# Two ordering edits in the first mixer of a hybrid decoder trunk: where a pair's normalised keys stand on VectorE, and when the second half's cosines and sines are loaded and scaled

## The chip, the cores and the metric

The kernel runs on one core of one Trainium2 chip. The metric is device time in microseconds (us) of one execution. The profile is one further execution under the hardware profiler, whose span runs from the first to the last instruction of the program.

## The reference, cut to what matters

The reference is a decoder trunk of two layers on a sequence of 1024 tokens with 1024 features, all in float32. The first layer mixes with two groups of heads: eight retention heads (rotary q and k) and eight RWKV-7 heads. Only that first mixer is touched.

```python
z = h @ w_in                                 # h = rms_norm(x)
q, k, v, g = jnp.split(z_ret, 4, axis=-1)    # retention heads
q = rotary(heads(q), pos)                    # x1*cos - x2*sin, x1*sin + x2*cos
k = rotary(heads(k), pos) * HEAD_DIM ** -0.5
o = chunk_retention(q, k, heads(v))
...
kkf = heads(kr * k_k)                        # RWKV heads: normalised keys
kk = kkf / jnp.maximum(jnp.linalg.norm(kkf, axis=-1, keepdims=True), 1e-12)
...
y = rwkv7_scan(r_h, heads(decay), k_h, v_h, -kk, kk * heads(a))
```

`rwkv7_scan` goes token by token; the kernel does it in chunks of 64 tokens, with a short recurrence from chunk to chunk. After the mixer come its output projection, a SwiGLU FFN, a layer of sliding-window attention with its own FFN, and a final norm.

## The kernel before

Features lie on the 128 partitions and tokens along the free axis, in two halves of 512 tokens. The RWKV heads go in pairs (two heads of 64 features fill 128 partitions). So (0,3) is the fourth pair of the first half, and a unit is two pairs of one half: units 0 and 1 are the first half's pairs 0, 1 and 2, 3; units 2 and 3 are the second half's.

**Projections.** A projection job is 24 matmuls of 128x512: eight slices of the features, three products each, since activations and weights are split into a rounded high part and a remainder (`n` and `w` in the profile). ScalarE makes a weight's high part (L335), in the mixer VectorE makes its remainder (L336). The activations `n` of the second half are made by `gained`: ScalarE multiplies a slice by its gain and rounds it (L469), VectorE makes the remainder (L470), for each of eight slices. The factor 1/rms (`rs`) is not in `n`; it is multiplied in when a result leaves PSUM. For the rotary projections it is multiplied into the cosines and sines instead, on GpSimd (L485 for the first half, L585 for the second).

**Rotary.** When a rotary projection (`retk`, `retq`) is done, ScalarE copies it out (L1013), four small DMAs fetch a copy with the halves swapped (L1017), GpSimd multiplies by the cosines (L1018), VectorE the copy by the sines (L1019) and adds them (L1020). The tiles `c_cos` and `c_sin` have one buffer each, so the second half's can be loaded only when the first half's last rotation has read the old ones.

**The second half's norm.** `second_norm` loads x, sums its squares and makes `rs` (L572, L573). Then it waits for the event `g0_3`, the end of the first half's last projection, loads the eight slices of x again (L579, four buffers `nq`), makes `n`, and last loads and scales cosines and sines. The second half's projections begin with `w1_0`.

**A pair.** `pair` makes the decays, the inverse norm of the keys (`rn`), and with L712 the normalised keys `kk`. Behind it on VectorE come seven more operations that need `kk` or what follows from it: L715, L716 (into AR), L717, L719, L723, L724 (into BK), L752. AR and BK feed a matmul whose masked result (L736) goes through DRAM into the unit's triangular inversion (L857 and L861, 31 steps of two small VectorE operations).

**The recurrence.** `unit` ends with eight steps, one for each chunk: eight small matmuls into one PSUM bank (`ps_c`), then for each of the two pairs one VectorE operation that writes the next state (L959). Matmuls of the outputs (`ps_m<-AR,GT`) use those states.

**What sets the order.** `Plan` is a planner in the kernel: it traces the pieces of these generators and the projection jobs in an order by estimated costs and due times; a `yield (("retq0_3", 1.0),), 0.0` means that a generator goes on one unit of the planner's clock behind the event `retq0_3`. The framework then orders each engine's and queue's instructions once more, ahead of time, by when their inputs are there in its own model; where several could go, the one traced first goes first. The order of each queue is then fixed. Two helpers tie it:

```python
def keep(self, i):
    return self.tc.keep_in_program_order(i)   # i goes behind the instruction traced just before it on its queue
def behind(self, i, first):                   # i goes behind first on their common engine
    self.tc.add_manual_dep(i.ins, first.ins.name, ...)
```

The eight loads of x at L579 are all tied with `keep`.

## Time and profile before

| | |
|---|---|
| time, median of 3 runs | 2331.51 us (2331.47 to 2333.43) |
| time of the profiled execution | 2330.62 us |
| span of the profile | 2328.6 us (2.0 us of the time lie around it) |
| TensorE busy | 98% of the span |
| VectorE, ScalarE, GpSimd busy | 73%, 45%, 42% |
| matmuls of the first mixer | from 5.7 us to about 660 us of the span |

PE is TensorE, DVE VectorE, ACT ScalarE, POOL GpSimd, and SPq the queue of SyncE, which issues nearly all DMAs. A row of the timeline gives the start in us, the time that its instructions took in us (the merged ones together, where it ends with x2 and the like), engine, line and operation, what it writes and reads, and in brackets the engine's idle time before it and what ended that. A row of the waits gives who waited for whom, the total in us, how often, and the longest. A row of the windows gives, for a stretch of the span, each engine's busy time and instructions, then the granted TensorE clock as a share of full speed, and the share and rate of the DMA engines.

### The profile page before, as it was taken

What the parts mean: (1) busy time and instruction counts of PE and PEld (TensorE: products, weight loads), DVE (VectorE), ACT (ScalarE), POOL (GpSimd) and SP (SyncE); (2) the same over time, 40 slices, a digit from 0 to 9 for tenths busy, and PEclk for the clock granted to TensorE, in tenths of its full rate; (3) what the DMA queues carried; (4) which work ended last, traced back from release to release, by engine and by line L of the source; (5) the groups of instructions that cost most, each with busy time, mean ns of one, the idle gap of its engine ahead of it and who ended that gap; (6) DMA issues with size and microseconds to landing.
All of it is one profiled execution on the core that took longest, in us unless ns stands there. A gap on an engine that the chain in (4) does not pass through costs nothing.

```text
span 2328.6 us, 35662 instructions
## 1 busy us (share of the span) xinstructions
PE 2289.3 (98%) x13056; PEld 1816.4 (78%) x13056; DVE 1704.2 (73%) x2667; ACT 1044.2 (45%) x1943; POOL 979.8 (42%) x764
## 2 busy tenths in 40 slices
PE   8999999999999999999999999999999999999998
PEld 6777777777778888888788887777788888887886
DVE  6876865875667358888885957877647788888766
ACT  5454434424455333333343456666645333343335
POOL 3132221211341067777776500002102677776775
PEclk9999999999999999999999999999999999999999
DMA  7665553433445555555666331113236466656663
GB/s 276 207 210 194 189 152 127 138 119 112 148 173 191 201 167 207 209 208 214 249 257 216 107 127 64 57 64 122 96 128 224 159 222 218 214 200 252 249 217 113
DMA packets 170622, 407.46 MB, mean 175 GB/s; under 512 B 43216, under 2 KB 45904, under 8 KB 170448
## 3 DMA queue, kind: packets, MB, share of 16 engines
q1 hardware_dynamic: 167040, 398.63, 49.9%
q10 hardware_dynamic: 2832, 4.45, 0.5%
q8 instruction: 104, 1.70, 0.3%
q0 software_dynamic: 576, 2.10, 0.2%
q14 instruction: 70, 0.57, 0.1%
HBM read 276.53 MB, written 123.21 MB: 172 GB/s over the span
## 4 chain that ended last, share of the span: by engine, by line
PE 69%; DVE 5%; ACT 2%; issue 1%; POOL 0%; DMA 0%; DVEq 0%; POOLq 0%; ACTq 0%
PE ps_m L1191 7%; PE ps_m L1192 7%; PE ps_m L1193 7%; PE ps_f L350 4%; PE ps_f L351 4%; PE ps_f L352 4%; PE ps_f L1191 4%; PE ps_f L1193 4%; PE ps_f L1192 4%; PE ps_r L1191 2%; PE ps_r L1193 2%; PE ps_r L1192 2%; PE ps_c L1193 2%; PE ps_c L1192 2%; PE ps_c L1191 2%; PE ps_m L240 2%
## 5 line engine op out<-in xcount | busy, mean ns | idle before, releaser
L240 PE MATMUL ps_f<-n,w 128*128 128x512 f32 x1440 | 379.3, 411 | 8.9 <-ACT w L335 5.7
L240 PEld LDWEIGHTS ps_f<-n,w 128*128 128x128 f32 x1440 | 266.6, 190 | 91.4 <-issue 21.8
L336 POOL TENSOR_TENSOR w<-wr,w 128x512 fp32r<-128x512 f32 x63 | 85.9, 1368 | 523.9 <-ACT w L335 520.1
L335 ACT CAST w<-wr 128x512 fp32r<-128x512 f32 x231 | 142.1, 619 | 178.0 <-PE ps_f L352 76.7
L336 DVE TENSOR_TENSOR w<-wr,w 128x512 fp32r<-128x512 f32 x168 | 120.7, 722 | 68.2 <-ACT w L335 67.9
L336 POOL TENSOR_TENSOR w<-wq,w 128x512 fp32r<-128x512 f32 x91 | 130.3, 1442 | 31.9 <-ACT w L335 31.9
L1191 PE MATMUL ps_m<-n,w 128*128 128x512 f32 x333 | 130.9, 393 | 0.0
L1193 PE MATMUL ps_m<-n,w 128*128 128x512 f32 x333 | 130.2, 391 | 0.4 <-POOL w L1379 0.4
L1192 PE MATMUL ps_m<-n,w 128*128 128x512 f32 x333 | 130.1, 391 | 0.0
L350 PE MATMUL ps_f<-n,w 128*128 128x512 f32 x320 | 127.3, 399 | 0.0
L1200 DVE TENSOR_TENSOR nq<-ps_m,u 128x512 f32<-128x512 f32 x88 | 58.9, 684 | 93.3 <-PE ps_m L1193 93.3
L351 PE MATMUL ps_f<-n,w 128*128 128x512 f32 x320 | 126.9, 396 | 0.0
L352 PE MATMUL ps_f<-n,w 128*128 128x512 f32 x320 | 126.6, 396 | 0.0
L1191 PE MATMUL ps_f<-n,w 128*128 128x512 f32 x287 | 113.7, 396 | 0.0
L1193 PE MATMUL ps_f<-n,w 128*128 128x512 f32 x287 | 112.1, 392 | 0.0
L1192 PE MATMUL ps_f<-n,w 128*128 128x512 f32 x287 | 111.7, 389 | 0.0
L358 POOL TENSOR_TENSOR n<-nq,n 128x512 fp32r<-128x512 f32 x60 | 100.0, 1677 | 7.6 <-ACT n L356 7.6
L1379 POOL TENSOR_TENSOR w<-wd,w 128x512 fp32r<-128x512 f32 (+1 forms) x62 | 85.1, 1379 | 38.9 <-ACT w L1378 37.2
L1191 PE MATMUL ps_m<-cb,w 128*128 128x512 f32 x236 | 91.9, 389 | 0.3 <-DVE nq L1200 0.3
L1379 POOL TENSOR_TENSOR w<-ws,w 128x512 fp32r<-128x512 f32 (+1 forms) x48 | 71.8, 1502 | 47.8 <-ACT w L1378 47.8
L1192 PE MATMUL ps_m<-cb,w 128*128 128x512 f32 x236 | 91.8, 389 | 0.0
L1193 PE MATMUL ps_m<-cb,w 128*128 128x512 f32 x236 | 91.8, 389 | 0.0
(520 smaller groups left out, 6456.9 us busy)
## 6 DMA issues: line engine op xcount, KB each, us to landing
hc<-n SPq DMA_DIRECT2D x84, 512.0 KB, 2.8
wsp<-w SPq DMA_DIRECT2D x54, 512.0 KB, 3.4
w<-wsp SPq DMA_DIRECT2D x54, 512.0 KB, 3.5
n<-hc SPq DMA_DIRECT2D x54, 512.0 KB, 5.6
wq<-in_w_gate SPq DMA_DIRECT2D x44, 512.0 KB, 4.4
u<-u SPq DMA_DIRECT2D x88, 256.0 KB, 3.1
wr<-in_w_in SPq DMA_DIRECT2D x34, 512.0 KB, 4.9
ha<-hc SPq DMA_DIRECT2D x34, 512.0 KB, 5.7
```

The lines of the kernel that those rows point to most:

```text
L240: self.nc.tensor.matmul(out, lhsT, rhs, **kw)
L335: nc.scalar.copy(hi[:, :n], raw[:, c])
L336: self.lo.tensor_tensor(out=lo[:, :n], in0=raw[:, c], in1=hi.bitcast(F32)[:, :n], op=ALU.subtract)
L350: nc.tensor.matmul(ps, hi, rh, start=k == 0, stop=False)
L351: nc.tensor.matmul(ps, hi, rl, start=False, stop=False)
L352: nc.tensor.matmul(ps, lo, rh, start=False, stop=k == n - 1)
L358: e.tensor_tensor(out=lo, in0=src, in1=hi.bitcast(F32), op=ALU.subtract)
L1191: mm(ps, hi, xh, start=first and k == 0, stop=False, skip_group_check=True)
L1192: mm(ps, hi, xl, start=False, stop=False, skip_group_check=True)
L1193: mm(ps, lo, xh, start=False, stop=last and k == len(w) - 1, skip_group_check=True)
L1200: self.last_add = V.tensor_tensor(out=o, in0=x, in1=y, op=ALU.add)
L1379: nc.gpsimd.tensor_tensor(out=lo, in0=v, in1=hi.bitcast(F32), op=ALU.subtract)
```

## The change

`unit` keeps the last L959 instruction that was traced, of whichever unit and step, in `self.link`. `pair` ties its L712 behind that instruction on VectorE, if there is one. And `second_norm` loads and scales the second half's cosines and sines in a step of its own, one unit of the planner's clock behind `retq0_3` (the first half's last rotary projection) and ahead of its wait for `g0_3`, where they stood behind the eight slices of `n`.

```diff
-        self.h, self.plan = [None, None], None
+        self.h, self.plan, self.link = [None, None], None, None
...
         nc.scalar.activation(r, r, AF.Exp, scale=-0.5)
+        yield (("retq0_3", 1.0),), 0.0
+        cs = []
+        for nm in ("cos", "sin"):
+            c = self.const(self.rp, nm, (HT, HT), eng=nc.sync)
+            nc.gpsimd.tensor_tensor(out=c, in0=c, in1=r, op=ALU.mult)
+            cs.append(c)
         yield (("g0_3", 0.0),), 0.0
         n8 = self.n8(self.pp)
         self.nT = []
...
             self.keep(nc.sync.dma_start(x, self.A["xT"][k, :, HT:T]))
             self.nT.append(self.gained(x, "n1a", n8, k))
         self.rs = r
-        cs = []
-        for nm in ("cos", "sin"):
-            c = self.const(self.rp, nm, (HT, HT), eng=nc.sync)
-            nc.gpsimd.tensor_tensor(out=c, in0=c, in1=r, op=ALU.mult)
-            cs.append(c)
         self.cs = cs
...
-        V.scalar_tensor_tensor(out=kk, in0=k, scalar=self.col("kk", p), in1=rn, op0=ALU.mult, op1=ALU.mult)
+        i = V.scalar_tensor_tensor(out=kk, in0=k, scalar=self.col("kk", p), in1=rn, op0=ALU.mult, op1=ALU.mult)
+        if self.link is not None:
+            self.behind(i, self.link)
...
-                V.scalar_tensor_tensor(
+                self.link = V.scalar_tensor_tensor(
                     out=self.Srw[:, p, :] if c == NCH - 1 else GT[:, c + 1, :], in0=ps[:, q, :],
```

## The prediction

> **What bounds the kernel now.** I read the first lines of the page, then PE's waits, then windows around the two waits that the change can touch, and last each engine's timeline there.

> ```profile
> span 2328.6 us, 35662 instructions
> PE 2289.3 (98%) x13056; PEld 1816.4 (78%) x13056; DVE 1704.2 (73%) x2667; ACT 1044.2 (45%) x1943; POOL 979.8 (42%) x764
> PE ps_f L240 <- DVE n L470: 2.1, 1, 2.1
> PE ps_m L240 <- DVE GT L959: 2.0, 1, 2.0
> ```

> PE is the bound: 2289.3 of 2328.6 us. Neither edit removes a matmul, so all that can be won is PE's idle time and what hangs on it. Two of its longest waits are the ones that the edits touch: PE waited 2.0 us for a recurrence step (L959) and 2.1 us for a slice of the second half's activations (L470).

> ```profile
> 203.88:207.29 3.41, 1.79 (x29) 1.62 (x30) 3.38 (x8) 0.00 (x0) 0.00 (x0) 1.00 0.38 154
> 207.29:210.70 3.41, 3.41 (x8) 2.30 (x7) 1.80 (x5) 0.62 (x1) 0.00 (x0) 0.50 0.00 0
> 285.80:289.21 3.41, 1.50 (x15) 0.90 (x11) 3.41 (x4) 3.34 (x7) 3.04 (x3) 1.00 0.33 88
> 289.21:292.62 3.41, 3.17 (x8) 2.49 (x9) 3.41 (x7) 0.00 (x0) 0.00 (x0) 0.50 0.86 291
> ```

> Windows of 3.41 us: PE's busy time first, DVE's third, the granted clock third from the end. Each wait is followed by 3.41 us at half the clock. So a wait costs twice: the idle time, and the slow matmuls behind it.

> ```profile
> 206.51 3.56 PE L240 MATMUL ps_f<-n,w 128*128 128x512 f32 x9
> 209.87 1.44 PE L240 MATMUL ps_m<-rr,c_blk 128*128 128x512 f32 x2
> 220.89 5.28 PE L240 MATMUL ps_f<-n,w 128*128 128x512 f32 x22
> 226.01 1.02 PE L240 MATMUL ps_m<-rt,c_blk 128*128 128x512 f32 x2
> 289.45 5.40 PE L240 MATMUL ps_f<-n,w 128*128 128x512 f32 x16 [2.15 <-DVE n L470]
> ```

> A projection matmul takes 5.28/22 = 0.24 us at full clock. Nine would take 2.16 but took 3.56 in the first slow window, and the two of `c_blk` 1.44 where 1.02 is usual: 1.8 us lost. Behind the second wait 16 took 5.40 where 3.84 is due: 1.56 us. The first wait is thus worth 2.0 + 1.8 = 3.8 us, the second 2.15 + 1.56 = 3.7.

> [...]

> **Part 1, the keys.**

> ```profile
> 201.29 0.40 PE L240 MATMUL ps_c<-GT,XA 64*64 64x64 f32 x8
> 202.89 0.91 DVE L336 TENSOR_TENSOR w<-wr,w 128x512 fp32r<-128x512 f32 x1 [2.48 <-ACT w L335]
> 203.72 0.74 DVE L712 SCALAR_TENSOR_TENSOR rt<-rkk,pv,rt 128x512 f32<-128x512 f32 x1
> 204.49 0.68 DVE L715 TENSOR_TENSOR AR<-rt,rt 128x504 f32<-128x504 f32 x1
> 205.17 0.47 DVE L959 SCALAR_TENSOR_TENSOR GT<-ps_c,PC,XA 128x64 f32<-128x64 f32 x2
> 205.50 0.45 PE L240 MATMUL ps_m<-AR,GT 64*64 64x64 f32 x6 [2.01 <-DVE GT L959]
> 207.96 0.75 DVE L752 SCALAR_TENSOR_TENSOR rr<-rr,pv,rkk 128x512 f32<-128x512 f32 x1
> 222.35 0.46 DVE L959 SCALAR_TENSOR_TENSOR Srw<-ps_c,PC,XA 128x64 f32<-128x64 f32 x2
> ```

> The step's matmuls were over at 201.69; its DVE operation started at 205.17, because pair (0,3)'s L712 and L715 (and the short L716) stood in front. The planner traces that L712 behind all eight steps of unit 0, so the tie holds it behind the step of 222.35. On DVE the step now follows L336, which ends at 203.80. Its first operation ends 0.3 us later and PE goes on at about 204.1 in place of 205.50: -1.4 us. With that, the first window's PE time is 1.79 + 1.4 = 3.2 of 3.41, and I take the slow window as gone: -1.8. Bounds: 0, if another operation takes the keys' place, to -3.8.

> What is added is the wait of L712. Queued behind it are L715, L716, L717, L719, L723, L724 and L752, which with it held DVE from 203.72 to 208.71, less 0.47 for the step between them: 4.5 us that move to 222.8 or later. Who needs them:

> ```profile
> 222.00:236.00 14.00, 14.00 (x61) 9.91 (x60) 9.88 (x17) 7.05 (x13) 3.88 (x4) 1.00 0.66 223
> 240.10 1.15 PE L240 MATMUL ps_m<-AR,BK 64*64 64x64 f32 x32
> 245.98 1.02 PE L240 MATMUL ps_m<-rr,c_blk 128*128 128x512 f32 x2
> 366.11 0.75 DVE L712 SCALAR_TENSOR_TENSOR rt<-rkk,pv,rt 128x512 f32<-128x512 f32 x1 [0.57 <-ACT rt L704]
> 398.89 0.80 DVE L715 TENSOR_TENSOR AR<-rt,rt 128x504 f32<-128x504 f32 x1
> ```

> AR and BK are first multiplied at 240.10, L752's result at 245.98. DVE was busy 9.88 of the 14 us behind the last step, so 4.1 us are free there; the 4.5 us fit by about 229, eleven us ahead of their use. I cost this at nothing; if the cover is gone (a weight remainder L336 queued behind the keys) it is one more stop like that of 205.50, 3.8 us. The other pair that the tie can move is (1,1), whose L712 ran at 366.11, ahead of unit 1's last steps; its AR waited until 398.89 anyway: nothing. The other pairs are traced ahead of any step, or long behind the last one: nothing. Part 1: -3.2 us.

> **Part 2, cosines and sines.**

> ```profile
> 281.78 0.68 DVE L336 TENSOR_TENSOR w<-wr,w 128x512 fp32r<-128x512 f32 x1
> 283.58 1.18 DVE L470 SCALAR_TENSOR_TENSOR n<-nq,pv,n 128x512 fp32r<-128x512 f32 x1
> 284.68 1.34 DVE L857 TENSOR_TENSOR xt<-X,DT 128x108 f32<-128x108 f32 x1
> 285.95 1.77 DVE L336 TENSOR_TENSOR w<-wr,w 128x512 fp32r<-128x512 f32 x1
> 290.76 0.74 DVE L470 SCALAR_TENSOR_TENSOR n<-nq,pv,n 128x512 fp32r<-128x512 f32 x1
> 284.17 1.72 POOL L585 TENSOR_TENSOR c_cos<-c_cos,rs 128x512 f32<-128x512 f32 x1
> 285.86 1.31 POOL L585 TENSOR_TENSOR c_sin<-c_sin,rs 128x512 f32<-128x512 f32 x1
> ```

> DVE was busy for the whole 3.41 us of the window of the wait. Beside GpSimd's two multiplications L336 took 1.77 us, against 0.68 at 281.78, and a tiny L857 took 1.34. The slices of `n` stood behind these. With the multiplications elsewhere about 2 us of DVE come back there, and the wait of 2.15 us and its 1.56 us of slow clock go: -3.7.

> But the step that is moved also issues two DMAs on SP's queue, and these now stand ahead of the x loads:

> ```profile
> 261.06 0.57 SPq L305 DMA_DIRECT2D wr<-in_w_in  x1
> 261.68 5.74 SPq L579 DMA_DIRECT2D nq<-in_xT  x4
> 276.69 2.63 SPq L579 DMA_DIRECT2D nq<-in_xT  x2
> 280.96 0.38 SPq L265 DMA_DIRECT2D c_sin<-in_cst  x1
> 276.61 1.80 POOL L1018 TENSOR_TENSOR r<-r,c_cos 128x512 f32<-128x512 f32 x1 [1.35 <-DMA r<-r]
> 279.73 0.68 DVE L1019 TENSOR_TENSOR r<-r,c_sin 128x512 f32<-128x512 f32 x1
> DMA to landing us min/median/max: 2.7/3.8/4.6
> ```

> The x loads are tied (`keep`) to whatever was traced just before them on SP. That was the weight load of 261.06, and four of them went right behind it. In the new order it is the load of `c_sin`, which cannot go before the last rotation has read the old sines: 279.73 + 0.68 = 280.41 here. Without the slices of `n` in front of it, that L1019 can run at about 277 (its input landed when the L1018 of 276.61 started); the old cosines are free at 278.41. So I place `c_cos` and `c_sin` at 278.5 and 278.9 and the first x load at 279.3. From there by the rows: landing 3.8, then ACT's and DVE's part of a slice, both taken at DVE's 0.74, so the first slice is there at 284.6 and the fourth, three times 0.74 behind it, at 286.8. The last four loads need those buffers: 286.8 + 3.8 + 1.5 = 292.1, and 0.8 for what GpSimd still slows makes 292.9. Before, the last slice was done at 290.76 + 0.74 = 291.50. So +1.4, if PE fills its wait for the first slice with the matmuls of the last retention pair, which then no longer come later. Part 2: -3.7 + 1.4 = -2.3. Bounds: -3.7; and at the other end, a second set of loads as slow as before (from 276.69 to 291.50, 14.8 us, counted from a first slice at 286.7 when `c_sin` goes at 280.96 as now): a last slice at 301.5, +10.

> **Sum.** -3.2 - 2.3 = -5.5 us on the profiled execution's 2330.62: 2325.1. The median of the runs stands 0.9 above that execution, so I say **2326.0 us**.

> **The rivals.**
> *Only the first edit pays (no change that can be told).* The x loads' later start eats what the freed DVE gives back; the second wait changes its name from L470 to the x load and keeps its price. For it: the four loads lose 17 us of lead. Or the tie moves nothing, since the next ready DVE operation fills the keys' place. -3.2 to 0: 2328.3 to 2331.5.
> *The x loads come too late (slower).* At the end of the first half's projections PE finds neither slices nor other matmuls. It decides from where the last slice is more than 8 us late, at 299.5 or later: then it costs more than part 1's 3.2 us and the 0.2% (4.7 us) together. At its end, +10 - 3.2 = +6.8: 2338.3. For it: SP's queue goes in order, so one waiting load holds up all behind it. Against: DVE is emptier by then, so the second set should take nearer 8 than 15 us.
> *The keys come too late (slower).* 4.5 us on DVE from 222.8 on make weight remainders late: +3.8 each, and the framework's fixed order behind them shifts. With two such stops and nothing won from part 2: +7.6 - 3.2 = +4.4 or more, 2336. Against: 4.1 us are free there.

> **How the numbers follow.** The forecast 0.47; only the first edit or nothing 0.19; x loads 0.24; keys 0.10. Faster or slower by 0.2% is 4.7 us, about what a measurement of this kernel can tell from no change. The forecast's own range is 2322.5 (both waits and clocks wholly gone, 7.5 us, and 1.5 more) to 2327.5, of which nearly all counts as faster; the x loads and the keys count as slower, but for a little that falls short. Faster 0.47, same 0.20, slower 0.33. The range 2322 to 2339 takes in all named ends and leaves out orders that come out worse still.

> **What would show it.** Right: PE's wait for L959 under 0.7 us, full clock at 204 to 211; L712 of (0,3) behind the eighth step; two L585 ahead of most L470; x loads behind `c_sin` on SP; no half clock near 290; the last L470 within 2 us of where it was, counted from the end of the last first-half projection. Wrong: PE waiting over 4 us for an x load or an L470, or for an L336 behind the keys; a new half-clock window in the mixer; or a different order of the later units with new waits of their own.

## The result: slower by 0.33%

The changed kernel took 2340.36 us (median; 2338.11 to 2343.25 in 9 runs) where the kernel before, beside it on the same chip, took 2332.15 us (2330.42 to 2338.15 in 9 runs). The ratio is 1.0033, with a 95% interval of 1.0024 to 1.0042: 7.7 us slower, where I had forecast 5.5 us faster. Line numbers of the changed kernel run a little ahead of those of before: L712 of the pair is L713 here, a recurrence step L962, the x loads L585, the scaling L578.

From the page of the changed kernel, span and PE:

```profile
span 2338.6 us, 35666 instructions
...
PE 2291.0 (98%) x13056; PEld 1817.8 (78%) x13056; DVE 1703.8 (73%) x2667; ACT 1044.5 (45%) x1943; POOL 978.3 (42%) x764
```

The work of no engine grew by more than 2 us: DVE is busy for 1703.8 us against 1704.2, PE for 2291.0 against 2289.3. What is new are PE's waits. Those of the changed kernel between 200 and 540 us (total, how often, longest):

```profile
PE ps_m L250 <- DVE GG L779: 4.2, 2, 2.6
PE ps_f L240 <- ACT n L469: 3.0, 1, 3.0
PE ps_m L240 <- DVE r L1070: 2.1, 2, 1.4
PE ps_m L240 <- DVE GT L962: 1.6, 2, 1.2
PE ps_m L240 <- issue: 1.4, 1, 1.4
```

The recurrence step and the slice of `n` are still in the list, with 1.2 and 3.0 us, and three other names have joined them. Rows of the changed kernel's timeline show both edits at work:

```profile
207.87 0.33 PE L240 MATMUL ps_m<-AR,GT 64*64 64x64 f32 x4 [1.17 <-DVE GT L962]
...
218.97 0.47 DVE L962 SCALAR_TENSOR_TENSOR Srw<-ps_c,PC,XA 128x64 f32<-128x64 f32 x2
219.35 0.74 DVE L713 SCALAR_TENSOR_TENSOR rt<-rkk,pv,rt 128x512 f32<-128x512 f32 x1
...
279.53 0.68 DVE L1022 TENSOR_TENSOR r<-r,c_sin 128x512 f32<-128x512 f32 x1
280.24 0.33 SPq L265 DMA_DIRECT2D c_sin<-in_cst  x1
281.10 1.37 SPq L585 DMA_DIRECT2D nq<-in_xT  x3
283.60 0.38 SPq L585 DMA_DIRECT2D nq<-in_xT  x1
290.76 2.69 SPq L585 DMA_DIRECT2D nq<-in_xT  x4
283.14 1.27 POOL L578 TENSOR_TENSOR c_sin<-c_sin,rs 128x512 f32<-128x512 f32 x1
284.37 1.30 POOL L578 TENSOR_TENSOR c_cos<-c_cos,rs 128x512 f32<-128x512 f32 x1
...
285.40 0.72 ACT L469 ACTIVATE n<-nq,pv 128x512 fp32r<-128x512 f32 x1
286.17 1.22 PE L240 MATMUL ps_f<-n,w 128*128 128x512 f32 x2 [3.00 <-ACT n L469]
288.84 1.51 PE L240 MATMUL ps_m<-r,r 128*64 128x64 f32 x18 [1.45 <-DVE r L1070]
290.00 2.06 DVE L470 SCALAR_TENSOR_TENSOR n<-nq,pv,n 128x512 fp32r<-128x512 f32 x3
297.46 0.74 DVE L470 SCALAR_TENSOR_TENSOR n<-nq,pv,n 128x512 fp32r<-128x512 f32 x1
```

The keys stand behind the eighth step (218.97), and PE's stop for the fifth step is 1.17 us instead of 2.01. (The steps are counted from one here. Some of the expectations below count from nought and call this stop that of the fourth step.) The x loads stand behind `c_sin`, which could go when L1022 had read the old sines, at 280.21. GpSimd's multiplications run at 283.14, nearly where they ran before (284.17). The first slice of `n` is not there when PE wants it (3.00 us), and the last is done at 298.20 instead of 291.50.

Windows of the changed kernel (PE's busy time first, the granted clock third from the end):

```profile
206.40:209.80 3.40, 2.23 (x51) 1.82 (x46) 1.76 (x5) 1.28 (x3) 0.67 (x1) 1.00 0.55 223
284.75:288.16 3.41, 1.22 (x2) 0.50 (x2) 3.41 (x5) 2.66 (x5) 2.60 (x2) 0.50 0.93 299
288.16:291.58 3.42, 2.74 (x28) 2.11 (x30) 3.42 (x7) 0.72 (x1) 0.00 (x0) 0.50 0.47 156
291.58:294.99 3.41, 3.41 (x17) 2.70 (x14) 2.48 (x8) 1.75 (x3) 0.00 (x0) 0.50 0.80 252
```

The half clock behind the fifth step is gone, as forecast. Where I had expected the other one to go, three follow each other.

Written out engine by engine, the programs before and after have the same instruction order up to the change, and again, but for a few exchanges on ScalarE, from the mixer's last part on. In between the framework has moved instructions on every engine; some 1,100 of PE's 10,948 matmuls stand at another place in its order. So I split this stretch at unit 1's first recurrence step, which I call the border, and added up for each part PE's idle time (gaps over 0.06 us) and what half clock cost it (half of PE's busy time in the half-clock windows, where the granted clock was 0.50). From the end of unit 0's fourth step to the border this was 8.1 us before and 13.3 after; from the border to unit 3's first step 8.3 before and 13.9 after. Together that is 10.8 us more. The time between the two outer steps grew by 8.4 us (from 414.3 to 422.7), and the median of the runs by 7.7. The second part lies behind everything that the edits name.

### The profile page after: what moved, and what is told of

Its sections match the earlier page's. It is cut to its first block, busy times and chain, and to the rows that moved or that the text cites. A ratio compares the mean times of both kernels' runs of the same rounds, so it can differ in the third digit from the quotient of the medians.

```text
span 2338.6 us, 35666 instructions
## 1 busy us (share of the span) xinstructions
PE 2291.0 (98%) x13056; PEld 1817.8 (78%) x13056; DVE 1703.8 (73%) x2667; ACT 1044.5 (45%) x1943; POOL 978.3 (42%) x764
## 4 chain that ended last, share of the span: by engine, by line
PE 76%; DVE 9%; ACT 3%; DMA 2%; issue 2%; POOL 1%; SPq 1%; DVEq 0%; POOLq 0%; ACTq 0%
PE ps_m L1194 7%; PE ps_m L1196 7%; PE ps_m L1195 7%; PE ps_f L240 6%; PE ps_m L240 4%; PE ps_f L350 4%; PE ps_f L351 4%; PE ps_f L352 4%; PE ps_f L1196 4%; PE ps_f L1194 4%; PE ps_f L1195 4%; PE ps_r L1194 2%; PE ps_c L1196 2%; PE ps_r L1196 2%; PE ps_c L1194 2%; PE ps_r L1195 2%
## 5 line engine op out<-in xcount | busy, mean ns | idle before, releaser
L240 PE MATMUL ps_f<-n,w 128*128 128x512 f32 x1440 | 377.7, 411 | 10.5 <-ACT w L335 6.0
L240 PEld LDWEIGHTS ps_f<-n,w 128*128 128x128 f32 x1440 | 266.3, 190 | 91.9 <-issue 20.6
L336 POOL TENSOR_TENSOR w<-wr,w 128x512 fp32r<-128x512 f32 x63 | 86.6, 1379 | 524.9 <-ACT w L335 521.0
L335 ACT CAST w<-wr 128x512 fp32r<-128x512 f32 x231 | 141.9, 618 | 181.7 <-PE ps_f L352 77.7
L336 DVE TENSOR_TENSOR w<-wr,w 128x512 fp32r<-128x512 f32 x168 | 117.7, 704 | 70.8 <-ACT w L335 70.4
L336 POOL TENSOR_TENSOR w<-wq,w 128x512 fp32r<-128x512 f32 x91 | 130.7, 1447 | 31.1 <-ACT w L335 31.1
```

What stands on the lines that cost most here:

```text
L240: self.nc.tensor.matmul(out, lhsT, rhs, **kw)
L335: nc.scalar.copy(hi[:, :n], raw[:, c])
L336: self.lo.tensor_tensor(out=lo[:, :n], in0=raw[:, c], in1=hi.bitcast(F32)[:, :n], op=ALU.subtract)
```

## The experiments

**Each edit alone.** The first kernel leaves out the second edit, the second kernel leaves out the first. The third and fourth have the keys' edit alone, too: the third ties only pair (0,3)'s keys, the fourth ties these behind the fifth step of unit 0 instead of the eighth. The lines that matter of the third and fourth:

```diff
 e3_keys_pair03
-        if self.link is not None:
+        if u == 1 and p == 3:
             self.behind(i, self.link)
 e4_keys_step4, with this too
+                if c <= 4:
+                    self.link = i
```

> Only the keys' tie; cosines and sines as before. Theory A (the x loads, tied behind the load of the sines, cost the time): the step's stop at about 204 shrinks, the half clock behind it goes, the last L470 comes as before: 1 to 3 us under before, at most no change. Rival B (the keys come too late, the second half's order shifts): +5 to +10 us here already, with stops of PE behind masked results (L779) near 261 and 429. Rival C (each edit costs its half): about +4.

> Only the earlier cosines and sines; the keys as before. Theory A: +5 to +9 us over before; on SP's queue all eight x loads behind the load of c_sin, the last L470 5 to 8 us later than 291.5, over 6 us of half clock between 284 and 296. Rival B: within 2 us of before. Rival C: about +4.

> The keys' tie for pair (0,3) alone. The program built with it differs from that with both ties only in VectorE's and ScalarE's order in a short stretch of the third unit. If the tie of pair (1,1) does nothing, as the prediction said: as the run with both keys tied, within 1 us. If the stops of the changed kernel near 429 to 442 come from (1,1): 2 to 4 us less than that run.

> The keys of pair (0,3) tied behind the fifth step (which the stop waited for) in place of the eighth. If what costs is only the lateness of the keys: the stop at 204 goes as with the whole tie, and nothing comes later: 3 to 4 us under before. If any change of the order there costs by its own: no better than the run with the whole tie.

Measured: the keys alone 1.0044 (1.0032 to 1.0057), cosines and sines alone 1.0043 (1.0031 to 1.0056), pair (0,3)'s tie alone 1.0047 (1.0034 to 1.006), the tie behind the fifth step 1.0019 (1.001 to 1.0028). Each edit alone costs about 10 us, as much as both together or more (the intervals overlap); the two costs do not add up. That speaks against two separate delays, and for something that comes out anew in each version. Pair (1,1)'s tie does nothing that can be told, as I had said. PE's waits in the kernel with the keys' tie alone, from 400 to 530 us:

```profile
PE ps_c L240 <- DVE GT L961: 3.6, 2, 3.3
PE ps_c L240 <- DVE TZ L886: 3.2, 3, 2.0
PE ps_m L240 <- DVE UV L821: 2.7, 1, 2.7
```

These stops lie over 200 us behind the keys. In the part behind the border stops and half clock are 20.6 us here, against 8.3 before; in the part ahead of it 7.9, against 8.1.

**The order held.** To part the edit from the order that came with it, a function called behind the trace of the kernel ties listed instructions of each engine one behind the other. A tie sets the order on an engine; it is of the class `NoSync`.

```diff
+def hold(tc, nc):
+    ins = nc.cur_bb.bb.instructions
+    for text in HELD.values():
+        seq = [ins[int(x)] for x in text.split()]
+        for a, b in zip(seq, seq[1:]):
+            tc.add_manual_dep(
+                b, a.name,
+                mybir.DependencyInfo(mybir.DependencyClass.NoSync, mybir.DependencyReason.DATA), reason="hold",
+            )
...
         trunk(tc, A, out)
+        hold(tc, nc)
```

The first of the four holds the whole mixer in the order of before, except the nine operations of pair (0,3)'s keys (eight on VectorE, one on ScalarE); the other three hold the order of before only from the border on.

> Only pair (0,3)'s nine key operations (L713 to L727 and L755) stand behind the eighth step; every other instruction of the mixer is held, on every engine, in the order of the kernel before. Theory (the later order that the framework deals anew is what costs): PE's stop for the fourth step and the half clock behind it go, nothing takes their place: 2328 to 2330.5, -2 to -4 against before. Rival (the keys themselves come too late, whatever the order): the cost of the keys' edit alone stays, +5 or more, 2338 or later, with PE waiting on operations behind the keys.

> The tie of pair (0,3)'s keys, with the order that it gave up to unit 1's first step, and from there on the order of the kernel before on every engine. Theory: PE's stops and half clock summed to 9.5 us between unit 0's fourth step and unit 1's first (before 8.1) and to 18.9 from there to unit 3's first step (before 8.3); with the later order of before the second sum goes back to about 8: 2332 to 2335, 0 to +2 against before. Rival (lateness of the keys is passed on through whatever order follows): the stops at 430 to 520 us stay, +8 or more: 2340 or later.

> Cosines and sines moved, with the order that this gave up to unit 1's first step, and from there on the order of the kernel before. Theory: two parts. The late loads of x cost here, ahead of unit 1 (stops and half clock there sum to 14.1 us against 8.1): +5 to +6 stays; the 7 us of stops and half clock behind that go with the order of before: 2337 to 2339. Rival A (all of the 10 us is the late loads and what they push back): 2341 to 2343. Rival B (all of it is the later order): 2332 to 2333.

> Both edits (the keys' tie for pair (0,3)), with their own order up to unit 1's first step, then the order of the kernel before. Theory: the stops and half clock ahead of unit 1 (13.3 us against 8.1) stay, those behind it (13.9 against 8.3) go: +3 to +5, 2335 to 2337. Rival A (lateness passed on): as the changed kernel, 2340. Rival B (the later order alone): 2332 or less.

Measured: the keys with the order of before 0.9992 (0.9983 to 1.0001); the keys with the later order of before 1.0014 (1.0004 to 1.0023) where the keys alone had 1.0047; cosines and sines with the later order of before 1.0029 (1.0018 to 1.004); both 1.0023 (1.0014 to 1.0033). The keys' lateness itself costs nothing that can be told. The timeline of the kernel with the keys moved and all else held:

```profile
207.22 0.45 PE L240 MATMUL ps_m<-AR,GT 64*64 64x64 f32 x6 [0.67 <-DVE GT L961]
...
222.41 0.46 DVE L961 SCALAR_TENSOR_TENSOR Srw<-ps_c,PC,XA 128x64 f32<-128x64 f32 x2
222.79 0.74 DVE L712 SCALAR_TENSOR_TENSOR rt<-rkk,pv,rt 128x512 f32<-128x512 f32 x1
```

The stop for the fifth step is 0.67 us, and the keys run from 222.79 on. From the end of the fourth step to that of the eighth it takes 19.4 us against 22.4: 3.0 us less, where I had priced 3.2. And PE's waits in the kernel with the keys' own order up to the border and that of before behind it, from 400 to 530 us:

```profile
PE ps_m L250 <- DVE XA L935: 1.1, 1, 1.1
PE ps_m L250 <- DVE GG L778: 1.1, 1, 1.1
```

These are the first of that list; the waits of 3.3, 2.0 and 2.7 us are gone with the later order that held them. The ratio fell by 0.0033; the 0.0014 that stay go with the order up to the border, and where they lie its profile doesn't show (7.9 us of stops and half clock there, as before). The profiled execution is one of the fastest of this kernel (2327.16 us, its median 2334.32), so I take the verdict from the ratio and from the profile only the names. For the second edit 0.0029 stays: that is another cost, ahead of the border.

**The new order without any edit.** The kernel before, its own order up to the border, and from there on the order that pair (0,3)'s tie had brought.

> No edit of the kernel at all: the order of the kernel before up to unit 1's first step, and from there on the later order that the keys' tie had brought (that of e3_keys_pair03). Theory (that order by itself costs): e3 less e6, +6 to +9 against before, 2337 to 2340, with PE's stops on VectorE between 400 and 530 us as in e3. Rival (the later order only looks bad because it follows on keys that came late): -1 to +2, 2330 to 2333.

Measured: 1.0048 (1.0035 to 1.0061). Nothing is edited and nothing comes late here, and the whole loss of the keys' edit is there. The timeline shows how such an order loses time:

```profile
514.09 0.45 PE L240 MATMUL ps_c<-GT,XA 64*64 64x64 f32 x8 [0.59 <-DVE GT L959]
...
515.44 0.69 DVE L1034 SCALAR_TENSOR_TENSOR r<-r,r 128x512 f32<-128x512 f32 x1 [1.32 <-ACT r L1033]
516.05 1.35 DVE L861 TENSOR_TENSOR X<-X,xt 128x100 f32<-128x100 f32 x1
...
516.93 0.45 PE L240 MATMUL ps_m<-r,r 128*64 128x64 f32 x8
...
519.91 0.28 DVE L857 TENSOR_TENSOR xt<-X,DT 128x120 f32<-128x120 f32 x1
520.11 0.47 DVE L959 SCALAR_TENSOR_TENSOR GT<-ps_c,PC,XA 128x64 f32<-128x64 f32 x2
...
520.72 0.69 PE L240 MATMUL ps_c<-GT,XA 64*64 64x64 f32 x8 [3.34 <-DVE GT L959]
```

The matmuls of a recurrence step are done at 514.54, and from 517.38 on PE has nothing else in its order. On DVE the step stands behind an L1034, for whose input DVE itself stood idle for 1.32 us, and then a run of small L861 and L857 of the triangular inverse, until 520.1. This is the same kind of stop as that at 205.50 in the kernel before, which the edit shortened, at another place and longer: 3.34 us.

**The x loads' lead.** Cosines and sines moved, with the order of before behind the border; but the first four x loads are tied behind the weight load, as before, and only the last four behind the sines. (`rawload` is the weight load, `sinload` the load of a constant, here the sines, that was traced last.)

```diff
-            self.keep(nc.sync.dma_start(x, self.A["xT"][k, :, HT:T]))
+            i = nc.sync.dma_start(x, self.A["xT"][k, :, HT:T])
+            if k < 4:
+                self.behind(i, self.rawload)
+            else:
+                self.behind(i, self.sinload)
```

> As e7_cs_tail, but the first four x loads are tied behind the weight load, as in the kernel before, and only the last four, which must wait for buffers anyway, stand behind the loads of cosines and sines. Theory (what costs in the second edit is that the first four loads lose their lead): stops and half clock ahead of unit 1 fall back to about 8 us, 2330 to 2333, 0 to +2 against before. Rival (the order of DVE's and PE's work around the moved multiplications, or the second four loads): +5 or more, 2336 to 2338, with PE waiting for slices after 284 us as in e7.

Measured: 0.9997 (0.9989 to 1.0006), against 1.0029 with all eight behind the sines. First the kernel with all eight, then that with four; SP's queue, PE's stops, and in the first the last addition of the rotation on DVE (L1020 in the kernel before):

```profile
283.02 0.33 SPq L265 DMA_DIRECT2D c_sin<-in_cst  x1
...
283.88 0.42 SPq L585 DMA_DIRECT2D nq<-in_xT  x1
...
284.83 1.46 SPq L585 DMA_DIRECT2D nq<-in_xT  x3
...
284.76 0.68 DVE L1021 TENSOR_TENSOR r<-r,r 128x512 f32<-128x512 f32 x1
285.54 2.32 PE L240 MATMUL ps_m<-r,r 64*128 64x128 f32 x16 [3.94 <-issue]
288.87 1.22 PE L240 MATMUL ps_f<-n,w 128*128 128x512 f32 x2 [1.01 <-ACT n L469]
```

```profile
266.63 5.78 SPq L585 DMA_DIRECT2D nq<-in_xT  x4
...
285.44 0.33 SPq L265 DMA_DIRECT2D c_sin<-in_cst  x1
285.86 1.81 SPq L585 DMA_DIRECT2D nq<-in_xT  x4
...
292.76 1.43 PE L240 MATMUL ps_f<-n,w 128*128 128x512 f32 x5 [1.16 <-DVE n L470]
295.31 1.66 PE L240 MATMUL ps_f<-n,w 128*128 128x512 f32 x6 [1.11 <-DVE n L470]
```

With all eight loads late, PE has no slice to multiply at 281.6. Next in its order are matmuls of the last retention pair, and these start 0.10 us after the last rotation is added, at 285.44: that is the stop of 3.94 us, for which the profile names no releaser. Then PE waits for the first slice.

With their lead back, the first four slices are there in time, and stops and half clock ahead of the border fall from 14.3 to 7.5 us. So of the second edit's 10 us, about 7 come with the first four loads' tie. How much of that is the later landing, and how much the order that the framework lays out around it, is not separated here. The other 3 are put down to the later order by difference (1.0043 against 1.0029), but the two intervals overlap. With the lead kept, the cosines' wait costs nothing that can be told.

The orders of two more programs settle what in the edit acts. With the second edit made but its x loads tied as before, every engine's order is that of the kernel before; and with only the two loads of cosines and sines moved and GpSimd's multiplications left in their place, it is that of the second edit. What the second edit does, it does through the tie.

**The keys one place earlier, and the kernel before again.** Keys behind the fifth step, all else held; and an unchanged kernel, to see what differs from one execution to the next.

> Pair (0,3)'s keys behind unit 0's fifth step instead of the eighth, with every other instruction of the mixer held in the order of the kernel before. Theory: the stop for the fourth step and the half clock behind it are worth the 3.2 us that I priced: 2327 to 2330, -1 to -3. Rival (a window at half clock that goes here comes at another stop instead, as e5_keys_held, which won only 0.6): 2329 to 2331, within 0.2%, with a half-clock window that the kernel before did not have.

> The kernel before, unchanged, for what one execution differs from another. If the half-clock window behind the fourth step is the stop's own doing, it is there again (204 to 211 us) with a stop of about 2.0 us; the time is 2329 to 2334. If windows and stops up to 0.7 us come and go by themselves, the sums of stops and half clock by stage differ by 1.7 us or multiples from the first profile.

Measured: 0.9992 (0.9983 to 1.0) and 1.0003 (0.9994 to 1.0011). The first bounds what moving the keys can bring by itself: at most 4 us, likeliest 2. From the second profile of the kernel before:

```profile
208.45 0.45 PE L240 MATMUL ps_m<-AR,GT 64*64 64x64 f32 x6 [2.00 <-DVE GT L959]
...
208.95:212.36 3.41, 3.41 (x26) 2.81 (x22) 3.09 (x7) 0.63 (x1) 0.00 (x0) 0.50 0.00 0
```

The stop for the fifth step (2.00 us) and the half clock behind it are there again (2.01 us and the window from 207.29 on in the first profile), so I take them to belong to the program. The half clock behind the slices of `n` is there, too (at 294.28 us). The half-clock windows at 593 and 2115 us of the first profile are not there, and there are two new ones at 461 and 1148.

**Both edits without their two costs.** Both edits, the first four x loads with their lead, the order of before around and behind the two places; keys behind the eighth step and, in the second kernel, behind the fifth.

> Both edits freed of the two costs found: pair (0,3)'s keys behind the eighth step, cosines and sines moved with only the last four x loads behind them, and the order of the kernel before held around the two places and behind them. If the forecast's working was right for the direct effects (-3.2 and -3.7): 2325 to 2328. If the stops that go are given back within the stages, as the single edits showed (-0.6 and -0.6): 2330 to 2333.

> As the run before it, with the keys behind the fifth step (the first place that leaves the fourth step free). By the direct effects 2325 to 2328; by the single edits' -2.3 and -0.6: 2328 to 2331, faster than both kernels by 0.1%.

Measured: 0.9993 (0.9983 to 1.0002) and 0.9992 (0.9983 to 1.0001), 2330.46 and 2330.15 us beside 2331.81. No version beats the kernel before by more than can be told, though all four that avoid the two costs and have the keys moved lie at 0.9992 or 0.9993. The direct effects of both edits together are between -4.0 and +0.5 us, likeliest -1.7; the -6.9 that I had for them (-3.2 and -3.7) is excluded.

## Why the prediction was wrong

**Part 1.** The direct steps held. The stop went from 2.01 to 1.17 us in the changed kernel (0.67 with the order held; I had 0.6), the half clock behind it went (in the changed kernel the granted clock was 1.00 from 86.8 to 284.7 us), and 4.5 us of keys behind the eighth step hid behind other work: between 222 and 284 us of the held kernel no wait of PE is over 0.6 us. Pair (1,1) was nothing. The step that failed is "I cost this at nothing": I asked who needs the moved operations, and not what the framework does with all that follows. I had the sentence, "the framework's fixed order behind them shifts", in the third rival, and made of it two weight remainders late at 3.8 us each, on the condition that the keys come late. The condition was wrong: they came early enough, and the order shifted all the same. Its price was about 11 us with the keys alone, and the new order costs that much without the keys (1.0048).

**Part 2.** The x loads went behind `c_sin` as I had worked out, and `c_sin` went at 280.24, 1.3 us behind my 278.9, though the eighth step had ended 3.4 us earlier than before: the last L1022 ran at 279.53, behind other operations of DVE's order, and not at about 277. I had the first slice at 284.6; ACT's part of it ended at 286.12 and released PE's two matmuls of 286.17, DVE's did not begin before 290.00, behind seven other operations of the fixed order, four of them the retention's. I had the last at 292.9; it came at 298.20. By my own measure, counted from the end of the last first-half projection (277.24 before, 279.63 now, the 720th matmul of the projections in both), the last slice is 4.3 us later than before, where I had 1.4, and the first one's remainder is 11.5 us later. The 0.8 us in that sum for what GpSimd still slows was my estimate, worked out from no row; the eight L470 of the changed kernel took 0.74 to 0.75 us each, where the longest of before took 1.77. The term that failed is "+1.4, if PE fills its wait for the first slice with the matmuls of the last retention pair": the retention's operations wait on DVE and GpSimd as well, and PE had a stop of 3.00 us for the slice and 1.45 behind it, with three half-clock windows in place of one. With the later order of before this costs 6.8 us (4.2 to 9.3), the rival *the x loads come too late* with its place and its sign.

Its threshold, a last slice more than 8 us late, was not reached: the last was 4.3 us late in the changed kernel, and 6.0 with the second edit alone and the later order of before. The stops that the profiles show are for the first slices; with the first four loads' lead back the last slice is 1.4 us late and the loss is gone. The rival's far end, 2338.3, is near the measured 2340.4, but in part by luck, for the later order that the edits brought has no term in that rival's sum.

The gain that I had set against it (-3.7) was not there either: in the kernel with the first four loads' lead two stops of 1.16 and 1.11 us, and one of 0.65 for an L336, stand in place of one of 2.15, and what went was the half clock.

**The sum.** Both edits together cost 7.7 us, either alone about 10; whether less or as much the intervals leave open. With the order of before behind the border both cost 5.4 us (3.3 to 7.7): part 2's late loads, less what the keys save. The other 2.3 I put down to the later order, by difference and not clear of noise; that a later order can cost this much and more is shown by the run that has nothing else (1.0048).

Not settled: by what rule the framework chose the orders, and so whether a given tie brings a good or a bad one. No trace shows that. Four versions (both edits, either alone, the keys behind the fifth step) brought four orders behind the border, with 13.9, 15.2, 15.5 and 20.6 us of stops and half clock there. The order of before had 5.4 to 11.2 us there in ten profiles, so the lowest of the four stands little above what one execution differs from another.

## What to carry to other kernels

Where a framework lays out a fixed order from ties and planned times, the price of one moved step is not only its own: compare the whole order of the two programs, and take the worth of what follows from the order that it brings, or hold that order. A load that is tied to "whatever was traced last" inherits the waits of what is put in front of it; ask what lead the first of them had, not when the last one lands. And a stop that vanishes from one place is won only if the waiting engine finds its next work in time: price the edit by the sum of stops over the whole stage.

## What the runs showed of the hardware

```profile
2111.93:2115.34 3.41, 1.09 (x4) 0.36 (x4) 3.41 (x5) 0.81 (x2) 0.93 (x2) 1.00 1.05 414
2115.34:2118.75 3.41, 3.41 (x9) 2.63 (x10) 3.41 (x3) 0.33 (x1) 3.17 (x2) 0.50 1.02 419
```

```profile
2117.02:2120.43 3.41, 1.63 (x7) 1.35 (x8) 3.41 (x5) 1.14 (x2) 1.60 (x2) 1.00 1.05 424
2120.43:2123.84 3.41, 3.41 (x17) 2.80 (x16) 3.41 (x4) 1.11 (x3) 2.13 (x3) 1.00 0.61 251
```

In the first the stop and a shorter one of 0.4 us ahead of it lie within one window, PE is busy for 1.09 us of it, and the next is at half clock; in the second the shorter one falls into the window ahead, PE is busy for 1.63 us, and the clock stays.

The profiles of the kernel before and of the changed kernel, divided on their own grids (670 windows each, between 20 and 2310 us), have five full-clock windows each in which PE was busy for less than 2.0 us:

| profile | followed by half clock, PE busy (us) | followed by full clock |
|---|---|---|
| before | 1.09, 1.50, 1.61, 1.79 | 1.63 (at 1142.54) |
| changed kernel | 1.25, 1.48, 1.79, 1.90 | 1.63 (at 424.70) |

All other full-clock windows of the two profiles were followed by full clock. The busy time alone does not decide: 1.63 us kept the clock where 1.79 and 1.90 did not.

At a granted clock of 0.50 a window of 3.41 us full of work loses 1.7 us, so by estimate a stop of 2 us is worth between 2.0 and 3.7 us. I had priced both at the upper end. For the fifth step's stop that held in both profiles of the kernel before (2.01 and 2.00 us); the stop of 1.9 us above had its half clock in one of the two.
